# An encoder layer on one core: four raw weight buffers, products ordered by their operands, the first pass woven into the left factors, token tiles one by one at the ends

## The chip, the core and the metric

The kernel runs on one core of one Trainium2 chip. The metric is the device time of one execution in microseconds. Times are given for several runs of a kernel, beside one execution that the hardware profiler recorded, from which every row of a profile in this text comes. TensorE (PE) does the matmuls, VectorE (DVE) the elementwise work, ScalarE (ACT) activations and casts, GpSimd (POOL) little here, and SyncE (SP) issues nearly all DMA transfers on one queue, in its program order. Each engine executes its own stream in order.

## The reference

One layer of a token-mixing encoder over 512 tokens of 2048 features, in fp32. A vector `mod` of six rows of 2048 is made from `c`. Four mixers of 512 features each (a gated recurrence, a diagonal state space, stick-breaking attention, a delta rule) work on one projection; their outputs are projected, and a gated feed-forward block follows. What this text is about is the second half:

```python
shift1, scale1, gate1, shift2, scale2, gate2 = split(silu(c) @ ada_w + ada_b, 6)
...
mix = concatenate([o_a, o_b, o_c, o_d], -1) @ w_out               # 2048 x 2048
x = layer_norm(ALPHA * x + gate1 * mix, ln1_g, ln1_b)
h = x * (1 + scale2) + shift2
ffn = (silu(h @ ffn_w1) * (h @ ffn_w3)) @ ffn_w2                  # 2048 -> 5632 -> 2048
out = layer_norm(ALPHA * x + gate2 * ffn, ln2_g, ln2_b)
```

## The kernel before, in words

**Numbers.** Every fp32 operand of a matmul is split into a high part, rounded by ScalarE (`copy`, L101), and a low part, the difference taken by VectorE (`sub`, L104 with all two-operand VectorE work). `mm3` makes a product of two such operands from three matmuls (L92): high by high, low by high, high by low. So each weight block goes through four hands: an SP load of the raw values, ScalarE's rounding `wh`, VectorE's difference `wl`, and TensorE.

**Order.** The program is written with a tile framework. A tile comes from a pool with a fixed number of buffers, and the framework puts in the waits: a load into a buffer waits for the last reader of what was there. Its scheduler puts the instructions of each engine in an order that follows the order of the code, except that what stands under `tc.high_priority(offset=...)` may be taken earlier by that offset (`E.ahead` is 500 for the weights; `soon`, 1500, for evictions). Pools opened on `E.low`, `E.high` and `E.psum` are given back in the middle of the program; what is opened after that takes over their space, and waits tile by tile for it.

**Heads and output projection.** The first 1035 us hold the input projection, the mixers and two parts of the output projection (`w_out` inside `body`: "W1" and "W2" of the order string). The last part, four of sixteen groups of 128 rows, takes what the stick-breaking attention gives. Its weights `wr` are loaded (L1469), multiplied by the gate row `g1` (a broadcast load, L1167) and split into `woh` and `wol`; then for each token tile t of 128 tokens, 4 x 4 x 3 matmuls into `pd`, additions into `acc`, and a layer norm (L1205, L1207). These weights are prepared after `E.high.close()`, with `g1` in the pool `tp`.

**Factors.** The up projection uses Strassen's scheme in Winograd's form: tokens in halves of 256, the 2048 features in halves of 1024, and the weight columns of `ffn_w1` and `ffn_w3` as the two column blocks. `feature` turns `acc` with 128x128 transposes (L95) into feature-major tiles; the loop over j = 0..7 (128 features of each half) forms the left factors a11, a12, a22 and the sums s1..s4, each split in two, which stay in 56 slots of 128x512. After all eight the 16 normalised tiles are stored to `xn` (L1532).

**Up projection.** 11 blocks n of 512 columns. A block has two passes over j. The first pass loads three raw 128x512 blocks into a tile `wx` of 128x4x512 (L1558) and does 18 matmuls, p1 with a11, p3 with s4, p2 with a12. The second loads four, makes three differences of them in place on VectorE, splits all four (`wb`, then `wa`) and does 24 matmuls: p1 with s2, p4 with a22 (both on `wb`), p7 with s3, p5 with s1 (both on `wa`). `wx` has two buffers (pool `fx`), `wh` and `wl` four each (pool `fh`). The gate's pieces u, v, g1, g2 are evicted under `soon`. In the first pass of the next block, behind j = 3, `turned` transposes the gated product g, splits it into `gh` and `gl` of 128x2x512 (two buffers each) and stores them to the scratch `gd` (L1579).

**Down projection.** Two halves r of 1024 output columns; 44 row tiles f of `ffn_w2` in pairs; each pair loads one `wx` of 1 MB and four pieces of `gh`, `gl` back from `gd` (L1680 to L1686), and does 48 matmuls, 12 for each of four token tiles in four accumulators `pt`. The first and the last pair of a half run token tile by token tile, the others row tile by row tile. During r = 0 VectorE computes the row `gate2` (`gate_steps`), and `gate_rows` broadcasts it. During r = 1 the residual is prepared (`base`), and each token tile then gets its gate, sum, layer norm and stores (L1723).

## Time and profile before

| what | value |
|---|---|
| runs | 2649.61 us median of three (2642.85 to 2654.33) |
| profiled execution, its own time | 2645.44 us |
| its span, first to last instruction | 2643.7 us |
| mean granted TensorE clock | 0.972 |
| last matmul of "W2" to first of the last output projection's steady run | 1034.9 to 1057 us |
| last output projection and layer norm | to 1106.8 us |
| left factors | to 1139.6 us |
| block 0: first pass, second pass | to 1174.4, to 1223.8 us |
| blocks 1 to 10 of the up projection | to 2114.3 us |
| down projection | to 2605.1 us |
| tail | to 2643.7 us |

Rows of the profile are read so. A row of groups has the line, engine and operation, the tiles as out<-in, the shape, how many; then busy us, mean ns of one; then the idle time of the engine just before them and what ended most of it. A row of waits has who waited, for whom, the us in all, how often, and the mean. A row of stretches has the window, its length, the busy us and count of PE, PEld, DVE, ACT and POOL, the granted clock, the DMA engines' busy share and GB/s. A row of the timeline has the start in us, the length, and the instruction. "SPq" is the DMA-issuing queue of SyncE. Lines L93 and up of the changed kernel are those of before plus one.

### The profile page before, as it was taken

To read this page: it belongs to the slowest core of one execution; us is meant where nothing else is said; L and a number is where in the kernel's file an instruction comes from. 1 tells how busy PE (TensorE), PEld (TensorE's weight loads), DVE (VectorE), ACT (ScalarE), POOL (GpSimd) and SP (SyncE) were. 2 spreads that over 40 slices of the span, in tenths; PEclk is the share of its full clock that TensorE was granted. 3 is DMA by queue.
4 is the path that set the end of the run, shared out by engine and by line. 5 is a ranking of instruction groups with operands and counts; after the bars stand their busy time and mean duration, and the time that the engine had idled before them with its cause. 6 is when DMAs were issued, how large, how long until landed. Compare 5 with 4: busy or idle time off the path is not lost.

```text
span 2643.7 us, 33043 instructions
## 1 busy us (share of the span) xinstructions
PE 2470.3 (93%) x11890; PEld 1885.3 (71%) x11890; DVE 1738.4 (66%) x2629; ACT 930.1 (35%) x1350; POOL 71.8 (3%) x193
## 2 busy tenths in 40 slices
PE   8999999999999997879999999999999999999994
PEld 3557767767888785667677777776777678888883
DVE  3856985566798747867767776677777655436226
ACT  2435342322545633253334343443443321121110
POOL 3200000100000000000000000000000000000000
PEclk9999999999999998889999999999999999999997
DMA  9876225336545442245466556555655878859531
GB/s 288 264 230 200 82 75 152 117 107 208 167 132 156 151 140 88 88 136 191 164 203 201 186 174 203 193 180 189 203 191 184 289 265 312 291 192 330 196 110 64
DMA packets 334572, 481.81 MB, mean 182 GB/s; under 512 B 44259, under 2 KB 150973, under 8 KB 334409
## 3 DMA queue, kind: packets, MB, share of 16 engines
q1 hardware_dynamic: 331672, 479.00, 55.6%
q8 instruction: 93, 1.52, 0.2%
q10 hardware_dynamic: 2256, 0.67, 0.1%
q14 instruction: 71, 0.57, 0.1%
q0 software_dynamic: 480, 0.05, 0.0%
HBM read 445.51 MB, written 34.10 MB: 181 GB/s over the span
## 4 chain that ended last, share of the span: by engine, by line
PE 26%; DVE 16%; DMA 12%; issue 6%; ACT 4%; SPq 2%; DVEq 0%; ACTq 0%
PE pt L92 18%; DMA wx<-in_ffn_w_dram 12%; PE pd L92 6%; DVE wl L104 6%; DVE wx L104 5%; ACT wh L101 3%; SPq L1558 2%; PE p L92 1%; DVE g L104 1%; DVE v L104 1%; DVE acc L122 0%; DVE y L122 0%; DVE wr L104 0%; DVE st L1205 0%; DVE wol L104 0%
## 5 line engine op out<-in xcount | busy, mean ns | idle before, releaser
L104 DVE TENSOR_TENSOR wl<-wx,wh 128x1024 fp32r<-128x1024 f32 (+1 forms) x440 | 475.1, 1115 | 387.2 <-ACT wh L101 385.3
L101 ACT CAST wh<-wx 128x1024 fp32r<-128x1024 f32 (+1 forms) x440 | 409.0, 965 | 877.9 <-PE pt L92 332.2
L92 PE MATMUL pt<-wh,gh 128*128 128x512 f32 x704 | 274.7, 390 | 0.0
L92 PE MATMUL pt<-wl,gh 128*128 128x512 f32 x704 | 274.4, 390 | 0.0
L92 PE MATMUL pt<-wh,gl 128*128 128x512 f32 x704 | 274.3, 390 | 0.0
L101 ACT CAST wh<-wr 128x512 fp32r<-128x512 f32 x236 | 145.8, 620 | 339.1 <-PE pd L92 233.2
L104 DVE TENSOR_TENSOR wx<-wx 128x512 f32<-128x512 f32 (+1 forms) x264 | 229.2, 868 | 42.9 <-DMA wx<-in_ffn_w_dram 37.2
L122 DVE SCALAR_TENSOR_TENSOR acc<-aw,cact,acc 128x512 f32<-128x512 f32 x240 | 179.9, 749 | 102.8 <-DMA aw<-in_ada_w_dram 99.6
L104 DVE TENSOR_TENSOR wl<-wr,wh 128x512 fp32r<-128x512 f32 x236 | 162.3, 691 | 127.6 <-ACT wh L101 106.1
L92 PE MATMUL pd<-hh,wl 128*128 128x512 f32 x512 | 206.6, 403 | 3.5 <-DVE wl L104 3.3
L92 PE MATMUL pd<-hh,wh 128*128 128x512 f32 x512 | 206.1, 404 | 2.4 <-ACT hh L101 2.4
L92 PE MATMUL pd<-hl,wh 128*128 128x512 f32 x512 | 205.1, 401 | 0.0
L92 PE MATMUL p<-wh,hdh 128*128 128x512 f32 x352 | 149.7, 425 | 31.9 <-ACT wh L101 22.6
L92 PE MATMUL p<-wh,hch 128*128 128x512 f32 x352 | 141.5, 402 | 13.9 <-ACT wh L101 13.9
L92 PEld LDWEIGHTS pt<-wh,gh 128*128 128x128 f32 x704 | 132.5, 188 | 28.2 <-ACT wh L101 0.8
L92 PEld LDWEIGHTS pt<-wl,gh 128*128 128x128 f32 x704 | 132.5, 188 | 27.7
L92 PEld LDWEIGHTS pt<-wh,gl 128*128 128x128 f32 x704 | 132.5, 188 | 27.2
L92 PE MATMUL p<-wl,hdh 128*128 128x512 f32 x352 | 143.1, 407 | 4.0 <-DVE wl L104 4.0
L92 PE MATMUL p<-wl,hch 128*128 128x512 f32 x352 | 139.6, 396 | 2.2 <-DVE wl L104 2.2
L92 PE MATMUL p<-wh,hdl 128*128 128x512 f32 x352 | 141.4, 402 | 0.0
L92 PE MATMUL p<-wl,hbh 128*128 128x512 f32 x352 | 139.8, 397 | 0.0
L92 PE MATMUL p<-wh,hbl 128*128 128x512 f32 x352 | 138.6, 394 | 0.0
(495 smaller groups left out, 4283.2 us busy)
## 6 DMA issues: line engine op xcount, KB each, us to landing
wx<-in_ffn_w_dram SPq DMA_DIRECT2D x616, 256.0 KB, 4.1
aw<-in_ada_w_dram SPq DMA_DIRECT2D x384, 256.0 KB, 4.3
wr<-in_w_in_dram SPq DMA_DIRECT2D x184, 256.0 KB, 3.1
wx<-in_ffn_w_dram SPq DMA_DIRECT2D x44, 1024.0 KB, 5.4
gh<-gd SPq DMA_DIRECT2D x88, 256.0 KB, 5.4
gl<-gd SPq DMA_DIRECT2D x88, 256.0 KB, 5.2
wr<-in_w_out_dram SPq DMA_DIRECT2D x64, 256.0 KB, 2.8
gd<-gh SPq DMA_DIRECT2D x22, 512.0 KB, 5.4
```

Of the source, the lines that this page charges most:

```text
L92: return self.nc.tensor.matmul(out=out, lhsT=lhsT, rhs=rhs, start=start, stop=stop, **kw)
L101: self.nc.scalar.copy(out=out, in_=in_)
L104: self.nc.vector.tensor_tensor(out=out, in0=a, in1=b, op=op)
L122: self.nc.vector.scalar_tensor_tensor(out=out, in0=a, scalar=s, in1=b, op0=op0, op1=op1)
L1558: nc.sync.dma_start(out=x[:, s], in_=i[w][0, 128 * k : 128 * k + 128, T * n : T * n + T])
```

## The change

1. **Last output projection.** `g1` is taken from the pool `ap` instead of `tp`, and `E.high.close()` moves behind this projection. The pool `tp` has 34 buffers instead of 35, `wh` becomes a pool of the whole program, and a pool `w1` of one buffer is new.
2. **xn.** Each token tile is stored right after its norm, not after the factors.
3. **Block 0.** The first pass of block 0 is done inside the loop of factors, with single blocks of 128x512, in the accumulators `pd` and `pm` of the heads. Factors of j + 1 are written ahead of the products of j. The slots of the factors are the pools hp, pp, w1, af and wh.
4. **Up projection.** `wx` has four buffers instead of two. Of a second pass, `wa` is split before `wb`, and the products are p7, p5 (on `wa`), then p6, p4 (on `wb`), except at j = 7, where the latter go first. `gh` and `gl` are single 128x512 tiles with one buffer each, stored one by one, in two calls of `turned` behind j = 2 and j = 4. u, v, g1, g2 have one buffer each.
5. **Down projection.** At the start of a half the first two pairs run token tile by token tile; in the first half the last block's `turned` stands between the tiles t = 1 and t = 2. At the end, the last two pairs of the first half and the last four of the second run token tile by token tile. The pool `fz` has 9 buffers and gets more from w1 and wh; `base` is done for a column block at once.

The diff, cut to its core:

```diff
-NT = 35
+NT = 34
...
-        self.wh = self.open(self.low, "wh", 3)
+        self.wh = pool("wh", 3)
+        self.w1 = pool("w1", 1)
...
-    E.high.close()
-    late = ExitStack()
-    E.ax = E.open(late, "ax", 8, side="right")
...
-        g1 = bcast(E, E.gate[2][0:1, T * n : T * n + T], "g1")
+        g1 = E.ap.tile([128, T], F32, name=E.nm("g1"), tag="aw")
+        nc.sync.dma_start(out=g1, in_=E.gate[2][0:1, T * n : T * n + T].rearrange("o n -> (o n)").partition_broadcast(128))
...
             E.ts(acc[t][n], acc[t][n], mu, ALU.subtract, rs, ALU.mult)
+            nc.sync.dma_start(out=xn[t, n], in_=acc[t][n])
+    E.high.close()
...
-    slots = [E.hp] * 32 + [E.pp] * 16 + [E.ax] * 8
+    slots = [(E.hp, "t")] * 32 + [(E.pp, "t")] * 16 + [(E.w1, "t"), (E.af, "t")] + [(E.wh, "wh"), (E.wh, "wl")] * 3
...
-    for j in range(8):
+    def factors(j):
         f, e = feature(j), feature(j + 8)
...
-    E.fx = E.open(ffn_w, "fx", 2)
-    E.f2 = E.open(ffn_t, "f2", 2)
...
+    def single(s, j):
+        with tc.high_priority(offset=E.ahead):
+            x = E.sb("wx")
+            nc.sync.dma_start(out=x, in_=block(s, j, 0))
+            if j < 3:
+                hi, lo = (E.wh.tile([128, T], F32R, name=E.nm(m), tag=m) for m in ("wh", "wl"))
+            else:
+                hi, lo = E.sb("wh", dt=F32R), E.sb("wl", dt=F32R)
+            E.copy(hi, x)
+            E.sub(lo, x, hi.bitcast(F32))
+        return hi, lo
+
+    p1, p3 = [E.psd(), E.psd()], [E.psd(), E.psd()]
+    p2 = None
+    factors(0)
+    for j in range(8):
+        w = list(zip(*[single(s, j) for s in (0, 2, 3)]))
+        if j < 7:
+            factors(j + 1)
+        p2 = p2 or [E.psm(), E.psm()]
+        first_pass(j, p1, p2, p3, w)
...
+    E.fx = E.open(ffn_w, "fx", 4)
+    E.f2 = E.open(ffn_t, "f2", 1)
...
-            hi, lo = two(E.f2, "gh", "gh", F32R), two(E.f2, "gl", "gl", F32R)
-            E.copy(hi, ps)
-            E.sub(lo, ps, hi.bitcast(F32))
-            k = 4 * n + 2 * h
+        for q in range(2):
+            hi, lo = (E.f2.tile([128, T], F32R, name=E.nm(m), tag=m) for m in ("gh", "gl"))
+            E.copy(hi, ps[:, q])
+            E.sub(lo, ps[:, q], hi.bitcast(F32))
             for s, t in enumerate((hi, lo)):
-                nc.sync.dma_start(out=gd[k : k + 2, s].rearrange("f p t -> p f t"), in_=t.bitcast(F32))
+                nc.sync.dma_start(out=gd[4 * n + 2 * h + q, s], in_=t.bitcast(F32))
...
+                if j in (2, 4):
+                    turned(*before, j // 2 - 1)
...
-                wb = parts(x[:, 2:4])
                 wa = parts(x[:, 0:2])
-            product(p1, A[j]["s2"], wb, 0, False, j == 7, skip_group_check=True)
-            product(p4, A[j]["22"], wb, 1, j == 0, j == 7)
-            product(p7, A[j]["s3"], wa, 1, j == 0, j == 7)
-            product(p5, A[j]["s1"], wa, 0, j == 0, j == 7)
+                wb = parts(x[:, 2:4])
+            ab = [(p7, "s3", wa, 1), (p5, "s1", wa, 0)]
+            cd = [(p6, "s2", wb, 0), (p4, "22", wb, 1)]
+            for p, a, w, c in cd + ab if j == 7 else ab + cd:
+                product(banks(p), A[j][a], w, c, j == 0 and (n == 0 or p is not p6), j == 7, skip_group_check=p is p6)
...
+        pairs = [pair_w2(f, r) for f in (0, 2)]
+        pt = []
+        for t in range(4):
+            if r == 0 and t == 2:
+                for h in range(2):
+                    turned(*before, h)
+            pt.append(bank2("pt"))
+            for p in pairs:
+                mm_w2(pt[t], t, p)
...
+        ends = range(NFT - 4, NFT, 2) if r == 0 else range(NFT - 8, NFT, 2)
...
+        pairs = [pair_w2(f, r, f < NFT - 4) for f in ends]
+        for t in range(4):
+            for p in pairs:
+                mm_w2(pt[t], t, p)
+            with soon():
...
```

Three places show how this moves instructions. The first is VectorE's stream at the end of "W2", where the last output projection is prepared: `go` and `acc` are W2's evictions, `wr` the raw weights times the gate row `g`, `wol` their low parts. Before:

```order
L104 TENSOR_TENSOR go_9539<-pd_9459,g_2042_9455 128x512
L104 TENSOR_TENSOR go_9542<-pd_9460,g_2042_9455 128x512
L104 TENSOR_TENSOR acc_8940<-acc_8940,go_9539 128x512
L104 TENSOR_TENSOR acc_8943<-acc_8943,go_9542 128x512
L104 TENSOR_TENSOR wr_9553<-wr_9553,g_2063_9551 128x512
L104 TENSOR_TENSOR wr_9560<-wr_9560,g_2063_9551 128x512
L104 TENSOR_TENSOR wr_9567<-wr_9567,g_2063_9551 128x512
L104 TENSOR_TENSOR wol_9557<-wr_9553,woh_9556 128x512
L104 TENSOR_TENSOR wr_9574<-wr_9574,g_2063_9551 128x512
L104 TENSOR_TENSOR wol_9564<-wr_9560,woh_9563 128x512
```

The change has this at the same place:

```order
L105 TENSOR_TENSOR wl_9521<-wr_9518,wh_9520 128x512
L105 TENSOR_TENSOR wol_9644<-wr_9640,woh_9643 128x512
L105 TENSOR_TENSOR wol_9651<-wr_9647,woh_9650 128x512
L105 TENSOR_TENSOR wol_9658<-wr_9654,woh_9657 128x512
L105 TENSOR_TENSOR go_9536<-pd_9460,g_2042_9458 128x512
L105 TENSOR_TENSOR go_9539<-pd_9461,g_2042_9458 128x512
L105 TENSOR_TENSOR acc_8937<-acc_8937,go_9536 128x512
L105 TENSOR_TENSOR acc_8940<-acc_8940,go_9539 128x512
L105 TENSOR_TENSOR go_9542<-pd_9462,g_2042_9458 128x512
L105 TENSOR_TENSOR go_9545<-pd_9463,g_2042_9458 128x512
L105 TENSOR_TENSOR acc_8943<-acc_8943,go_9542 128x512
L105 TENSOR_TENSOR acc_8946<-acc_8946,go_9545 128x512
```

Before, all 16 multiplications by the gate row and all 16 low parts stand behind the last evictions of W2; now all 16 multiplications and 12 of the low parts stand far ahead in the stream, before the stick-breaking weights, three low parts just before the last evictions and one right behind them.

The second place is VectorE's stream in a second pass: `wx<-wx` are the differences in place (one of 128x1024 and two of 128x512 for each j), `wl<-wx,wh` the low parts, two for each j; equal numbers of `wx` belong to one j. Before:

```order
L104 TENSOR_TENSOR wl_15504<-wx_15495,wh_15503 128x1024
L104 TENSOR_TENSOR wl_15508<-wx_15495,wh_15507 128x1024
L104 TENSOR_TENSOR wx_15535<-wx_15535 128x512 x2
L104 TENSOR_TENSOR wl_15544<-wx_15535,wh_15543 128x1024
L104 TENSOR_TENSOR wl_15548<-wx_15535,wh_15547 128x1024
L104 TENSOR_TENSOR wx_15575<-wx_15575 128x1024
L104 TENSOR_TENSOR wx_15575<-wx_15575 128x512 x2
L104 TENSOR_TENSOR wl_15584<-wx_15575,wh_15583 128x1024
L104 TENSOR_TENSOR wl_15588<-wx_15575,wh_15587 128x1024
```

Now:

```order
L105 TENSOR_TENSOR wx_13970<-wx_13970 128x1024
L105 TENSOR_TENSOR wl_13899<-wx_13890,wh_13898 128x1024
L105 TENSOR_TENSOR wl_13903<-wx_13890,wh_13902 128x1024
L105 TENSOR_TENSOR wx_13970<-wx_13970 128x512
L105 TENSOR_TENSOR wx_14010<-wx_14010 128x1024
L105 TENSOR_TENSOR wl_13939<-wx_13930,wh_13938 128x1024
L105 TENSOR_TENSOR wx_13970<-wx_13970 128x512
L105 TENSOR_TENSOR wx_14010<-wx_14010 128x512
L105 TENSOR_TENSOR wl_13943<-wx_13930,wh_13942 128x1024
L105 TENSOR_TENSOR wx_14010<-wx_14010 128x512
L105 TENSOR_TENSOR wx_14050<-wx_14050 128x1024
L105 TENSOR_TENSOR wl_13979<-wx_13970,wh_13978 128x1024
```

Before, the differences of a j stand right ahead of its own low parts; now differences of one or two later j stand between.

The third place is TensorE's stream in the left factors: `pm<-ident,acc` are the transposes, `pd` and `pm` with `wh` or `wl` the products of the first pass of block 0. Before, it had nothing but transposes here:

```order
L95 MATMUL pm_10013<-ident,acc_8421 128x128
L95 MATMUL pm_10048<-ident,acc_8421 128x128
L95 MATMUL pm_10020<-ident,acc_8769 128x128
L95 MATMUL pm_10055<-ident,acc_8769 128x128
L95 MATMUL pm_10083<-ident,acc_8412 128x128
```

Now the products of one j stand between the transposes of two factors:

```order
L93 MATMUL pm_10128<-wh_10089,hbh_10059 128x512
L93 MATMUL pm_10128<-wh_10089,hbl_10060 128x512
L93 MATMUL pm_10128<-wl_10090,hbh_10059 128x512
L93 MATMUL pm_10129<-wh_10089,hbh_10059 128x512
L93 MATMUL pm_10129<-wh_10089,hbl_10060 128x512
L93 MATMUL pm_10129<-wl_10090,hbh_10059 128x512
L96 MATMUL pm_10166<-ident,acc_8415 128x128
L96 MATMUL pm_10166<-ident,acc_8418 128x128
L96 MATMUL pm_10166<-ident,acc_8421 128x128
```

Each j brings 18 matmuls to this place, 144 in all, which stood behind all the transposes before.

More of the change, by code (lines that the diff above doesn't have):

```diff
@@ L1563, in product @@
             v = slice(128 * b, 128 * b + 128)
[L1564 to L1577 removed]
+            mm3(E, p[b], (a[0][:, v], a[1][:, v]), (w[0][c], w[1][c]), first, last, **kw)
@@ new lines, in body @@
+    p1, p3 = [E.psd(), E.psd()], [E.psd(), E.psd()]
[7 more added lines that the diff above has]
+        first_pass(j, p1, p2, p3, w)
+    u0, v, g1 = two(E.ft, "u"), two(E.ft, "v"), two(E.ft, "g1")
+    with soon():
+        for b in range(2):
+            E.copy(u0[:, b], p1[b])
+            E.copy(v[:, b], p3[b])
+            E.add(g1[:, b], u0[:, b], p2[b])
+            E.act(g1[:, b], g1[:, b], AF.Silu)
@@ new lines, in body, with parts, quad @@
+    E.low.close()
+    E.psum.close()
+    E.fh = E.open(ffn_w, "fh", 4)
+    E.fx = E.open(ffn_w, "fx", 4)
+    E.f2 = E.open(ffn_t, "f2", 1)
+    E.p2 = E.open(last, "p2", 4, space=PSUM)
+    bank2 = lambda name: E.p2.tile([128, 2, T], F32, name=E.nm(name), tag="p")
+    banks = lambda p: (p[:, 0], p[:, 1])
+    def parts(src):
+        hi, lo = two(E.fh, "wh", F32R), two(E.fh, "wl", F32R)
+        E.copy(hi, src)
+        E.sub(lo, src, hi.bitcast(F32))
+        return banks(hi), banks(lo)
+    def quad(j, n, which):
+        x = E.fx.tile([128, 4, T], F32, name=E.nm("wx"), tag="wx")
+        for s in which:
+            nc.sync.dma_start(out=x[:, s], in_=block(s, j, n))
+        return x
@@ new lines, in gate_rows, with base @@
+        for n in range(4):
+            g2[n] = bcast(E, E.gate[5][0:1, T * n : T * n + T], "g2", "fz")
+    cols = lambda m, n, name, p: bcast(E, i[m][0:1, T * n : T * n + T], name, p)
+    def base(n):
+        g, b = cols("ln1_g", n, "lg", "hp"), cols("ln1_b", n, "lb", "hp")
+        E.ts(g, g, ALPHA, ALU.mult)
+        E.ts(b, b, ALPHA, ALU.mult)
+        for t in range(4):
+            a = E.sb("acc", pool=E.pp if n >= 2 else E.fz)
+            nc.sync.dma_start(out=a, in_=xn[t, n])
+            E.mul(a, a, g)
+            E.add(a, a, b)
+            if n < 2:
+                E.mul(y0[t][n], y0[t][n], g2[n])
+                E.add(y0[t][n], y0[t][n], a)
+                a = y0[t][n]
+            acc[t][n] = a
```

265 lines of the change are left out of this document (118 added, 147 removed).

## The prediction

> **What bounds the kernel now.** I read the page first, then a table of the stretches of the second half of the program, then the waits and the groups of its longest stretch.
>
> ```profile
> PE 2470.3 (93%) x11890; PEld 1885.3 (71%) x11890; DVE 1738.4 (66%) x2629; ACT 930.1 (35%) x1350; POOL 71.8 (3%) x193
> ...
> wx<-in_ffn_w_dram SPq DMA_DIRECT2D x616, 256.0 KB, 4.1
> ...
> gd<-gh SPq DMA_DIRECT2D x22, 512.0 KB, 5.4
> ```
>
> TensorE's 93% does not say that nothing can be won: its matmuls overlap, so a row of late ones still looks busy. The distance between the starts of two matmuls is the better measure. The chain of waits has a stretch in which TensorE alone sets the time:
>
> ```profile
> 2126.66 238.03 PE pt L92 x1050
> ```
>
> That is 238.03 / 1050 = 0.2267 us a matmul, which I use as its price. Now the stretches (busy us and count of PE, PEld, DVE, ACT, POOL, then clock, DMA share, GB/s):
>
> ```profile
> 900.00:1000.00 100.00, 96.03 (x446) 79.65 (x445) 52.56 (x83) 41.00 (x68) 0.00 (x0) 0.98 0.45 147
> 1035.20:1057.00 21.80, 3.29 (x5) 1.15 (x4) 21.80 (x38) 11.39 (x20) 0.00 (x0) 0.62 0.00 0
> 1057.00:1106.80 49.80, 46.62 (x202) 38.26 (x202) 38.75 (x96) 0.52 (x2) 0.00 (x0) 0.95 0.17 64
> 1106.80:1139.60 32.80, 13.99 (x52) 8.91 (x51) 30.65 (x67) 28.34 (x51) 0.00 (x0) 0.50 0.23 80
> 1139.60:1174.40 34.80, 34.63 (x144) 27.88 (x144) 18.50 (x21) 13.96 (x18) 0.00 (x0) 0.95 0.60 197
> 1174.40:1223.80 49.40, 46.43 (x193) 36.90 (x194) 39.10 (x41) 19.76 (x20) 0.00 (x0) 0.97 0.49 159
> 1223.80:2114.30 890.50, 835.60 (x3521) 640.26 (x3519) 646.17 (x658) 353.70 (x389) 0.00 (x0) 0.98 0.59 197
> 2114.30:2605.10 490.80, 484.30 (x2137) 400.05 (x2136) 203.23 (x239) 99.35 (x99) 0.00 (x0) 0.99 0.66 229
> 2605.10:2643.70 38.60, 0.17 (x1) 0.00 (x0) 35.15 (x88) 0.00 (x0) 0.00 (x0) 0.53 0.29 109
> ```
>
> The rows are: the heads, the preparation of the last output projection, that projection with its layer norm, the left factors, the first pass of block 0, its second pass, blocks 1 to 10 of the up projection, the down projection, and the tail after the last matmul. Three of them are VectorE's alone (1035 to 1057, 1106.8 to 1139.6, 2605 to the end). The longest is blocks 1 to 10: 3360 matmuls in 890.5 us, where 3360 x 0.2267 = 762 us would do.
>
> ```profile
> ACT wh L101 <- DVE wx L104: 288.7, 80, 4.8
> DVE wl L104 <- ACT wh L101: 183.4, 115, 5.1
> ACT wh L101 <- DMA wx<-in_ffn_w_dram: 154.6, 65, 8.0
> PEld p L92 <- ACT wh L101: 86.7, 147, 1.9
> PE p L92 <- ACT wh L101: 38.2, 82, 1.5
> ...
> PE p L92 <- DVE g L104: 9.0, 8, 1.5
> ...
> SPq L1558 <- DVE wl L104: 540.3, 155, 8.9
> ```
>
> Here is the ring: the load queue waits for VectorE's last read of a raw block (540 us), ScalarE waits for the load and for VectorE's differences, VectorE for ScalarE's rounding, and TensorE's weights for both. No engine in it is full (VectorE 646 of 890 us); two raw buffers make them take turns.
>
> **The change part by part.** A to F are in order of time. TensorE's matmuls are the same in number.
>
> **A, the last output projection's preparation.**
>
> ```profile
> 1034.93 0.39 PE L92 MATMUL pd<-wl,cath 128*128 128x512 f32 x1
> ...
> 1038.20 1.89 DVE L104 TENSOR_TENSOR wr<-wr,g 128x512 f32<-128x512 f32 x3
> ...
> 1058.02 0.63 PE L92 MATMUL pd<-woh,cath 128*128 128x512 f32 x1
> 1058.45 0.63 PE L92 MATMUL pd<-woh,catl 128*128 128x512 f32 x1
> ```
>
> Three of these multiplications take 1.89 us at 0.69 each, so they follow at 0.60. The 16 multiplications, 16 subtractions and 4 more for the left operand, 36 x 0.60 = 21.6 us, all stand behind the projection before, and TensorE gets four matmuls done from 1035.2 to 1057. In the order of the change all 16 multiplications and 12 of the 16 subtractions come earlier; of the last four, three stand before the last evictions and one behind. What covers them: in 900:1000 VectorE is busy 52.6 of 100 us. Gone are 21.8 less four matmuls (0.9), and some cold matmuls (0.43 apart at 1058 instead of 0.23). If the earlier place costs all that it saves the gain is 0; at best 22. I take 20, since the cover is more than twice the work: **-20**.
>
> **B, factors and first pass of block 0.**
>
> ```profile
> 1106.77 0.78 ACT L98 ACTIVATE hf<-pm,h2b,h2s 128x512 f32<-128x512 f32 x1 [49.28 <-PE pm L95]
> ...
> 1115.83 0.43 DVE L104 TENSOR_TENSOR hr<-hf,hf 128x256 f32<-128x256 f32 x1
> ...
> 1119.57 0.43 DVE L104 TENSOR_TENSOR hr<-hf,hf 128x256 f32<-128x256 f32 x1
> ```
>
> One factor step is 3.74 us of VectorE (1115.83 to 1119.57), eight are 30. Then the first pass takes until 1174.4: 67.6 us from the first factor. Now each step also splits three blocks, 3 x 0.60 on VectorE: 5.54 us, against 18 x 0.2267 = 4.1 us of TensorE and 8 transposes (52 of them fill 14.0 us at the half clock of that stretch, 0.27 each: at most 2.2 a step, half of it warm). So VectorE paces: 8 x 5.54 + 1.3 at the start + 4.1 for the last pass = 49.7; with 2.3 for handing on between three engines, 52: **-15.6**. Bounds: 49.7 (-18), and no overlap of the two at all (0). The 24 single loads stand behind the 16 xn stores on SP's queue, as the loads did before. [...]
>
> **C, second pass of block 0.** 49.4 us now against 192 x 0.2267 = 43.5. Its raw buffers take over the space of the tiles of B, so its first quad has to land (4.1), be subtracted and rounded (about 1.2 and 1.0) after B: 43.5 + 6.3 = 49.8. **0**, between -6 and +4 (one landing more).
>
> **D, blocks 1 to 10.**
>
> ```profile
> 1313.96 0.39 PE L92 MATMUL p<-wh,ha 128*128 128x512 f32 x1
> ...
> 1351.98 0.51 PE L92 MATMUL p<-wh,hdh 128*128 128x512 f32 x1 [0.30 <-ACT wh L101]
> ...
> 1402.51 0.63 PE L92 MATMUL p<-wh,ha 128*128 128x512 f32 x2
> ```
>
> First matmuls of a first pass, of its second pass, and of the next block: 38.0 and 50.5 us. At TensorE's price 8 x 18 x 0.2267 = 32.6 (35.0 with 16 transposes, 2.4) and 8 x 24 x 0.2267 = 43.5. What the feeders need for the second pass:
>
> ```profile
> L104 DVE TENSOR_TENSOR wl<-wx,wh 128x1024 fp32r<-128x1024 f32 x240 | 286.2, 1223 | 183.8 <-ACT wh L101 183.4
> ...
> L104 DVE TENSOR_TENSOR wx<-wx 128x512 f32<-128x512 f32 x160 | 110.7, 692 | 5.1
> ...
> L104 DVE TENSOR_TENSOR wx<-wx 128x1024 f32<-128x1024 f32 x80 | 97.7, 1222 | 33.0 <-DMA wx<-in_ffn_w_dram 32.9
> ...
> L95 PE MATMUL tr<-ident,g 128*128 128x128 f32 x16 | 2.4, 275 | 0.0
> ```
>
> (The last row is of one block, 1322 to 1410.) A quad is 3 x 1.22 + 2 x 0.69 = 5.0 us of VectorE against 24 x 0.2267 = 5.4 of TensorE. Before, its order was three differences and two subtractions in a row, each subtraction behind a rounding (183 us of waits); now differences of later quads stand between. Four buffers give a load three quads, 16 us, for its 4 issues and 4.1 us of landing. The demand, 56 loads of 256 KB per block, is 188 GB/s at 78 us a block; 229 were moved over the down projection. So TensorE paces: 76.2 + 2.4, and at each of two seams the wait for an eviction, 9.0 / 8 = 1.1: **81 us a block instead of 89.05, -80.5**. Bounds: -104 without any stall, 0 if the ring stays. I stay near the first, because all feeders fit in TensorE's time. The stores of gh and gl go from 4 of 512 KB to 8 of 256 a block, through one buffer instead of two: 4 pieces in a first pass of 35 us, each held for at most its landing of 5.4, 21.6 in all, fit.
>
> **E, down projection.**
>
> ```profile
> 2121.01 1.09 PE L95 MATMUL tr<-ident,g 128*128 128x128 f32 x4 [6.50 <-DVE g L104]
> ...
> 2364.61 1.07 PE L92 MATMUL gr<-acc,ones 128*32 128x512 f32 x8
> ```
>
> The last transposes wait 6.5 us for the gate; now two token tiles of the first two pairs (48 matmuls, 10.9 us) come first. 2112 x 0.2267 + 2.4 + 1.1 (eight small matmuls of the gate row) + 2 = 484.3 instead of 490.8: **-6.5**, between -8 and +8 (a landing and a half at the ends, where 32 tiles must be loaded).
>
> **F, tail.**
>
> ```profile
> 2597.15 1.29 DVE L104 TENSOR_TENSOR go<-pt,g 128x512 f32<-128x512 f32 x2 [11.51 <-PE pt L92]
> ...
> 2637.34 0.17 DVE L117 TENSOR_SCALAR lnr<-lnr 128x1 f32<-128x1 f32 x1
> ...
> 2638.87 1.41 DVE L122 SCALAR_TENSOR_TENSOR acc<-acc,lnr,lb 128x512 f32<-128x512 f32 x2
> ```
>
> Four token tiles now queue up behind 48 matmuls (10.9 us); VectorE takes from 2597.15 to 2640.3 for them, 10.8 us each. With four pairs to a tile the matmuls of one tile take 10.9 us, so VectorE just keeps step and one tile is left behind the last matmul. Its chain: six operations of 512 at 0.60, the aggregate 0.3, eight scalings at 0.66 (two take 1.41 at 0.75) and a dozen small ones at 0.2, with 0.3 for the start 11.9; and 3.4 from the end of the last VectorE operation (2640.3) to the span's end: 15.3 instead of 38.6: **-23.3**. Bounds -25 and, if VectorE lags 3 us a tile, -14.
>
> Sum: -20 - 15.6 + 0 - 80.5 - 6.5 - 23.3 = -145.9, from the profiled execution's 2645.4 (span 2643.7): 2499.5. Its time lies 4 us under the median of the three runs, which is inside their spread; I forecast **2500**. The heads, whose order shifts a little, get +-6.
>
> **Rivals.**
>
> 1. *VectorE and ScalarE keep the pace in D*: a second pass has 8% of room (5.0 of 5.4), and one rounding that comes late eats it. For it: 183 us of such waits. Against: other work now stands between. Half of D: 2500 + 40 = **2540**.
> 2. *The change does not do what it says in D*: the loads stay tied, by SP's one queue, in which a gd store that waits for its single gh buffer holds every load behind it, or ScalarE is held by that buffer with all roundings behind. For it: 5.4 us a store. Against: the old queue had such stores too, and its long waits are for VectorE. D is gone: **2580**.
> 3. *B runs at half clock.* Row for it: 0.50 granted in 1106.8:1139.6, and matmuls 0.43 apart at 1058. Then B is 144 x 0.43 + 64 x 0.27 = 79 instead of 52: **2527**. Against: TensorE has 4.1 us of matmuls in each 5.5. [...]
> 4. *Slower*: VectorE executes in order, and the multiplications of A now stand in the heads' time, before the stick-breaking weights; if they wait there for late gate rows or tiles, everything behind waits, and TensorE after it. The price is the wait itself; from 160 us it makes the kernel slower than before, say **2660**. Against: 900:1000 shows TensorE at 96 and VectorE half idle.
>
> **How the numbers follow.** Chances: forecast 0.60 (its own range 2465 to 2530, from the bounds of A, D and F), rival 1 0.17, rival 2 0.12, rival 3 0.08, rival 4 0.03. 2465 to 2555 holds the forecast's cases, rivals 1 and 3: 0.85 of the chance, less its edges. A measurement of this kernel can tell about 0.5% from no change; faster than that are all but rival 4 and some mishap on top of rival 2: 0.95, within it 0.02, slower 0.03.
>
> **What would show it.** A: no hole of 20 us before the last projection. B: about 52 us from the first factor to the second pass. D: starts of blocks 81 us apart, ScalarE's waits for DMA near zero. E: no wait of 6 us at the first down matmuls. F: 15 us after the last matmul. Wrong is the forecast if blocks stay above 86 us, or the heads end more than 10 us later.

## The result and the profile after

The changed kernel takes 2544.99 us, median of four runs (2540.67 to 2553.21), against 2646.23 us before in its company: a ratio of 0.9622, 95% interval 0.9579 to 0.9666. It is 101 us faster, where 146 were forecast; its profiled execution took 2540.67 us. The page's first rows, and the stretches that answer to those of before:

```profile
span 2539.0 us, 33233 instructions
...
PE 2422.7 (95%) x11890; PEld 1890.3 (74%) x11890; DVE 1733.9 (68%) x2665; ACT 946.5 (37%) x1386; POOL 77.2 (3%) x193
```

```profile
1042.40:1086.20 43.80, 43.80 (x195) 36.21 (x194) 35.47 (x83) 0.63 (x1) 0.00 (x0) 1.00 0.20 73
1086.20:1155.30 69.10, 46.31 (x210) 34.20 (x208) 53.25 (x110) 45.02 (x80) 0.00 (x0) 0.93 0.48 157
1155.30:1201.30 46.00, 45.50 (x192) 37.17 (x193) 40.83 (x44) 18.45 (x19) 0.00 (x0) 0.96 0.58 193
1201.30:1934.00 732.70, 710.24 (x3169) 581.77 (x3168) 576.76 (x613) 334.68 (x370) 0.00 (x0) 1.00 0.63 207
...
2028.90:2520.60 491.70, 485.69 (x2137) 399.95 (x2135) 221.63 (x297) 96.97 (x102) 0.00 (x0) 0.99 0.66 224
2520.60:2539.00 18.40, 0.21 (x1) 0.00 (x0) 13.77 (x32) 0.00 (x0) 0.00 (x0) 0.64 0.31 114
```

The rows are the last output projection, factors with the first pass of block 0, its second pass, blocks 1 to 9 (732.7 / 9 = 81.4 each), the down projection and the tail. Left out between is block 10, 1934.0 to 2028.9: 94.9 us, as against 81.4. By stage, in us of the two profiled executions:

| stage | before | after | moved | forecast |
|---|---|---|---|---|
| heads, to W2's last matmul | 1034.9 | 1042.4 | +7.5 | 0 (+-6) |
| A: from there to the first transpose of the factors | 66.7 | 43.8 | -22.9 | -20 |
| B: to the second pass of block 0 | 72.8 | 69.1 | -3.7 | -15.6 |
| C: second pass of block 0 | 49.4 | 46.0 | -3.4 | 0 |
| D: blocks 1 to 10 | 890.5 | 827.6 | -62.9 | -80.5 |
| E: down projection | 490.8 | 491.7 | +0.9 | -6.5 |
| F: tail | 38.6 | 18.4 | -20.2 | -23.3 |
| sum | 2643.7 | 2539.0 | -104.7 | -145.9 |

A and B are cut here at the first transpose of the factors (1101.6 us before, 1086.2 after). Cut at the first factor, as the forecast did it, B went from 67.6 to 64.1 us, where 52 were forecast.

The waits of blocks 1 to 9 (who waited for whom, us in all, how often, longest) show what became of the ring. The last figure of such a row is the longest wait, in the rows above too, where it was described as the mean:

```profile
ACT wh L102 <- PE p L93: 292.8, 215, 2.4
DVE wl L105 <- ACT wh L102: 93.3, 80, 1.5
DVE wx L105 <- DMA wx<-in_ffn_w_dram: 44.1, 35, 3.3
...
ACT wh L102 <- DMA wx<-in_ffn_w_dram: 1.5, 2, 0.7
```

ScalarE, which in blocks 1 to 10 waited 289 us for VectorE and 155 for loads, now in blocks 1 to 9 waits 293 us for TensorE and 1.5 for loads: ScalarE stands ready, and TensorE sets the time. VectorE's 44 us of waits for loads hardly reach it: its weights wait 0.8 us for `wl` there.

The runs had four questions: which part of the change carries D; what holds block 10; what B was short of; and where the heads lost 7.5 us. A and F were undone singly. The kernels of the experiments ran in four groups, each beside the kernel before, whose median there lies between 2644 and 2651 us; a difference of medians between two groups is therefore good to some 5 us, and the times of single stages, each read from one profiled execution, carry the readings.

### The profile page after: what moved, and what is told of

It is laid out like the page before. It is cut to its first block, busy times and chain, and to the rows that moved or that the text cites. A ratio compares the mean times of both kernels' runs of the same rounds, so it can differ in the third digit from the quotient of the medians.

```text
span 2539.0 us, 33233 instructions
## 1 busy us (share of the span) xinstructions
PE 2422.7 (95%) x11890; PEld 1890.3 (74%) x11890; DVE 1733.9 (68%) x2665; ACT 946.5 (37%) x1386; POOL 77.2 (3%) x193
## 3 DMA queue, kind: packets, MB, share of 16 engines
q8 instruction: 93, 1.52, 0.2%
## 4 chain that ended last, share of the span: by engine, by line
PE 53%; DVE 4%; DMA 3%; ACT 2%; issue 1%; SPq 0%; DVEq 0%; ACTq 0%
PE p L93 29%; PE pt L93 17%; PE pd L93 6%; DMA wx<-in_ffn_w_dram 2%; DVE wl L105 1%; ACT wh L102 1%; PE tr L96 1%; DVE gl L105 1%; DVE wx L105 0%; DVE acc L123 0%; SPq L1608 0%; DVE y L123 0%; DMA gd<-gl 0%; DVE st L1206 0%; ACT hf L99 0%
## 5 line engine op out<-in xcount | busy, mean ns | idle before, releaser
L102 ACT CAST wh<-wx 128x1024 fp32r<-128x1024 f32 (+1 forms) x444 | 421.5, 953 | 700.9 <-PE p L93 348.8
L105 DVE TENSOR_TENSOR wl<-wx,wh 128x1024 fp32r<-128x1024 f32 (+1 forms) x444 | 481.5, 1096 | 285.8 <-ACT wh L102 280.6
L93 PE MATMUL pt<-wh,gh 128*128 128x512 f32 x672 | 263.1, 392 | 6.0 <-DVE gl L105 6.0
L93 PE MATMUL pt<-wh,gl 128*128 128x512 f32 x672 | 262.6, 391 | 0.0
L93 PE MATMUL pt<-wl,gh 128*128 128x512 f32 x672 | 262.5, 391 | 0.0
L93 PE MATMUL p<-wh,hch 128*128 128x512 f32 x336 | 133.4, 397 | 13.4 <-ACT v L102 7.9
L93 PE MATMUL p<-wh,hbh 128*128 128x512 f32 x336 | 131.8, 392 | 8.5 <-DVE gl L105 8.5
L93 PE MATMUL p<-wh,hdh 128*128 128x512 f32 x352 | 137.1, 393 | 1.9 <-ACT u L102 1.0
L93 PE MATMUL p<-wl,hch 128*128 128x512 f32 x336 | 131.8, 392 | 0.5 <-DVE wl L105 0.5
L93 PE MATMUL p<-wl,hbh 128*128 128x512 f32 x336 | 131.6, 392 | 0.0
```

Of the source, the lines that this page charges most:

```text
L93: return self.nc.tensor.matmul(out=out, lhsT=lhsT, rhs=rhs, start=start, stop=stop, **kw)
L102: self.nc.scalar.copy(out=out, in_=in_)
L105: self.nc.vector.tensor_tensor(out=out, in0=a, in1=b, op=op)
```

## Experiments: what carries D

**Two raw buffers again.**

```diff
-    E.fx = E.open(ffn_w, "fx", 4)
+    E.fx = E.open(ffn_w, "fx", 2)
```

> The changed kernel with two raw buffers (pool fx) instead of four, all else as changed. If the number of raw buffers is what broke the ring of D, blocks 1 to 10 go back to about 88 us each from 82.7, and the time to about 2600. If the order of the products and of the differences did it, the blocks stay within 1 us of 82.7 and the time within 10 us of 2545.

2555.94 us, ratio 0.9672 (0.9648 to 0.9696): 11 us more than the change. Blocks 1 to 9 take 83.3 us each. With the new order, two buffers are nearly as good as four.

**The old order of a second pass.**

```diff
-                wa = parts(x[:, 0:2])
                 wb = parts(x[:, 2:4])
+                wa = parts(x[:, 0:2])
...
-            for p, a, w, c in cd + ab if j == 7 else ab + cd:
+            for p, a, w, c in cd + ab:
```

> The changed kernel with the old order in a second pass (wb split before wa, products p6, p4, p7, p5 at every j), still with four raw buffers. If the raw buffers carry D, blocks stay at 82 to 84 us and the time below 2560. If the order carries it, each second pass goes back towards 50 us from 45 and the time to about 2595.

2545.88 us, ratio 0.9628 (0.9612 to 0.9643), blocks of 81.6 us: no difference to the change. So with four buffers the order was not needed either, and neither run tells what carries D. The two had to be undone together.

**Both undone.** The two edits above in one kernel.

> The changed kernel with two raw buffers and the old order of a second pass together. Each alone cost little (blocks of 83.3 and 81.6 us). If either is enough to break the ring, both undone bring the blocks back to 87 to 89 us and the time to about 2610. If something else in the change does it (the transposed product taken in two calls and in single pieces, the evictions), the blocks stay below 85 us and the time below 2575.

2600.76 us, ratio 0.9815 (0.9788 to 0.9843). The eight blocks from 1294.0 to 1997.3:

```profile
1294.00:1997.30 703.30, 658.76 (x2817) 507.03 (x2817) 520.32 (x545) 284.30 (x328) 0.00 (x0) 1.00 0.59 192
```

703.3 / 8 = 87.9 us a block, against 88.9 before: the ring is back. What the rest of the change does in these blocks (transposes in two calls, single pieces, one buffer each) is 1 us a block at most, which two profiled executions can't tell from nothing (the run with the factors two steps ahead, below, shows why). Its waits beside those of the run with only the buffers undone, of stretches of eight blocks both; first both undone:

```profile
ACT wh L102 <- DVE wx L105: 220.1, 63, 5.1
DVE wl L105 <- ACT wh L102: 134.2, 82, 4.7
ACT wh L102 <- DMA wx<-in_ffn_w_dram: 126.0, 48, 7.3
PEld p L93 <- ACT wh L102: 64.7, 122, 1.7
```

And two buffers with the new order:

```profile
ACT wh L102 <- DVE wx L105: 155.0, 85, 5.0
ACT wh L102 <- DMA wx<-in_ffn_w_dram: 136.8, 59, 6.8
DVE wl L105 <- ACT wh L102: 89.2, 45, 4.3
```

With two buffers the loads come as late as ever (137 us of ScalarE's waits against 126). What the order takes away is the wait for the differences (220 to 155) and for the roundings (134 to 89), and TensorE's own 65 us of waiting for `wh`, of which 0.9 are left. That fits the code: `wa` needs only the first of three differences, so the first twelve matmuls of a j can be fed while the other two are made. That the twelve, and not VectorE's order as such, do it, was not separated.

**The order alone, in the kernel before.**

```diff
-                wb = parts(x[:, 2:4])
                 wa = parts(x[:, 0:2])
-            product(p1, A[j]["s2"], wb, 0, False, j == 7, skip_group_check=True)
-            product(p4, A[j]["22"], wb, 1, j == 0, j == 7)
-            product(p7, A[j]["s3"], wa, 1, j == 0, j == 7)
-            product(p5, A[j]["s1"], wa, 0, j == 0, j == 7)
+                wb = parts(x[:, 2:4])
+            ab = [(p7, "s3", wa, 1), (p5, "s1", wa, 0)]
+            cd = [(p1, "s2", wb, 0), (p4, "22", wb, 1)]
+            for p, a, w, c in cd + ab if j == 7 else ab + cd:
+                product(p, A[j][a], w, c, j == 0 and p is not p1, j == 7, skip_group_check=p is p1)
```

> The kernel before with only the new order of a second pass (wa split before wb, products p7, p5, p6, p4, at the last j the other way round); two raw buffers, all else as before. If the order alone breaks the ring, second passes fall from 51 to 43 to 46 us, blocks from 89 to 81 to 84, and the time to 2590 to 2600 (faster by 2%). If it needs the rest of the change, blocks stay above 87 and the time within 15 us of before.

2585.05 us, ratio 0.9749 (0.9723 to 0.9775). Nine blocks from 1217.6 to 1965.4:

```profile
1217.60:1965.40 747.80, 721.11 (x3169) 579.29 (x3169) 585.59 (x594) 326.19 (x351) 0.00 (x0) 1.00 0.62 203
```

747.8 / 9 = 83.1 us. A few lines that change no amount of work and no memory take 66 us from the kernel before, two thirds of what the whole change takes. The order and the buffers are two cures for one ring, and either alone is enough: the order alone in both kernels (83.1 and 83.3 us a block), the buffers alone in the changed kernel (81.6; in the kernel before they were not run alone). That both together bring more (81.4) is not clear of the differences between executions.

## Experiments: block 10 and the single store buffers

The timeline of SP's queue in the second pass of block 10 of the changed kernel, and VectorE's there:

```profile
1981.87 1.76 SPq L1608 DMA_DIRECT2D wx<-in_ffn_w_dram  x4
1983.72 0.38 SPq L1688 DMA_DIRECT2D gl<-gd  x1
...
1990.14 1.76 SPq L1608 DMA_DIRECT2D wx<-in_ffn_w_dram  x4
1992.00 0.38 SPq L1688 DMA_DIRECT2D gl<-gd  x1
1992.47 0.38 SPq L1688 DMA_DIRECT2D gh<-gd  x1
1992.90 0.42 SPq L1623 DMA_DIRECT2D gd<-gl  x1
```

```profile
1979.42 0.68 DVE L105 TENSOR_TENSOR gl<-tr,gh 128x512 fp32r<-128x512 f32 x1
...
1995.67 2.68 DVE L105 TENSOR_TENSOR wx<-wx 128x1024 f32<-128x1024 f32 x3 [4.96 <-DMA wx<-in_ffn_w_dram]
1998.88 0.69 DVE L105 TENSOR_TENSOR gl<-tr,gh 128x512 fp32r<-128x512 f32 x1 [0.53 <-DMA gd<-gl]
```

```profile
1999.72 0.76 PE L93 MATMUL p<-wh,hbh 128*128 128x512 f32 x1 [8.35 <-DVE gl L105]
```

The third piece `gl` of block 9 is made at 1979.4, but its store is issued only at 1992.9. Ahead of it in SP's queue stand loads of `gh` and `gl` for the down projection, and loads of two more quads `wx`, which in their turn wait for a raw buffer. From 1967 to 2002 the queue waits 9.5 us for VectorE's last reads of raw blocks and only 2.2 us for the slots of left factors that `gh` and `gl` take over. The fourth piece needs the buffer of the third, waits for that store, and holds the accumulator in which the product with a22 is to begin: TensorE starts it at 1999.7 after 8.35 us. Two holds end almost together there: on VectorE the fourth piece stands behind differences whose quad, issued at 1990.1 from the same queue, comes 5 us late, and the store's landing adds 0.5.

**These loads behind the stores.**

```diff
-        with tc.high_priority(offset=E.ahead):
-            x = E.fx.tile([128, 2, 2, T], F32, name=E.nm("wx"), tag="wx")
...
+        gg = []
+        with tc.high_priority(offset=E.ahead if r or f > 16 else 60):
+            for q in range(2):
+                hi, lo = E.sb("gh", dt=F32R, pool=E.hp), E.sb("gl", dt=F32R, pool=E.hp)
+                for s, t in enumerate((hi, lo)):
+                    nc.sync.dma_start(out=t.bitcast(F32), in_=gd[f + q, s])
+                gg.append((hi, lo))
+        with tc.high_priority(offset=E.ahead):
+            x = E.fx.tile([128, 2, 2, T], F32, name=E.nm("wx"), tag="wx")
```

> The changed kernel with the loads of gh and gl for the first pairs of the down projection placed later on SP's queue, behind the stores of the block before. If those loads, queued ahead of stores on which a single buffer waits, make the last second pass 61 us instead of 45, it goes to 46 to 48 and the time falls by 10 to 14 us. If the single buffers alone do it, or the banks, it stays above 58.

2531.02 us, ratio 0.9576 (0.9557 to 0.9596): 14 us less than the change. Block 10:

```profile
1947.10:2029.30 82.20, 79.01 (x353) 64.39 (x353) 64.74 (x69) 37.63 (x42) 0.00 (x0) 1.00 0.85 284
```

82.2 us instead of 94.9, like the others, while the DMA engines moved no less (284 GB/s; in the change 247 in the first pass and 288 in the second), so it is not the bandwidth. The place of these loads in the queue was the cause; the single buffers handed it on. Whether more buffers, with the loads left where they were, would have done as well was not run.

**Three edits read by stage.** The later loads; one rotating pool of three for `gh` and `gl`; and, for B, the low parts of block 0's first pass on GpSimd.

```diff
-    E.f2 = E.open(ffn_t, "f2", 1)
+    E.f2 = E.open(ffn_t, "f2", 3)
...
-            hi, lo = (E.f2.tile([128, T], F32R, name=E.nm(m), tag=m) for m in ("gh", "gl"))
+            hi, lo = (E.f2.tile([128, T], F32R, name=E.nm(m), tag="g") for m in ("gh", "gl"))
...
-            E.sub(lo, x, hi.bitcast(F32))
+            nc.gpsimd.tensor_tensor(out=lo, in0=x, in1=hi.bitcast(F32), op=ALU.subtract)
```

> Three local edits of the changed kernel, read by stage: the later loads of gh and gl as in the run before; gh and gl from one pool of three buffers instead of one buffer each; in the first pass of block 0 the low parts of the single weight blocks on GpSimd instead of VectorE. Blocks: if the single buffers still cost something, 82 falls towards 80. Start of the down projection: gaps of 8 us between its first matmuls fall to about 3 if the single buffers make them. B: if VectorE sets its pace (5.4 us of work and 1.1 of handing over in a step of 6.5), a step without the three low parts falls to about 5.3 us, ScalarE's pace, and B by 8 us; if the handing over between engines does, or GpSimd is slower than the step, B stays or grows. Time about 2520 if all three hold, 2530 if none but the first.

2521.08 us, ratio 0.9507 (0.9477 to 0.9538). Blocks 1 to 9 take 79.9 us instead of 82.0, and the down projection 486.5 instead of the 489.3 of the later loads alone (491.7 in the change). The changed kernel has these waits at its third and fourth token tile, whose accumulators the transposes had held:

```profile
2045.18 0.77 PE L93 MATMUL pt<-wh,gh 128*128 128x512 f32 x1 [3.49 <-DVE gl L105]
2054.78 0.70 PE L93 MATMUL pt<-wh,gh 128*128 128x512 f32 x1 [2.52 <-DVE gl L105]
```

So the single buffers do cost: about 2 us a block and 3 in the down projection. The three profiled kernels with three buffers have blocks of 79.9 to 80.1 us, the six with single ones and four raw buffers 81.4 to 83.0. B went the other way, from 69.1 to 77.8 us:

```profile
1109.66 4.80 POOL L1569 TENSOR_TENSOR wl<-wx,wh 128x512 fp32r<-128x512 f32 x3 [0.63 <-ACT wh L102]
```

GpSimd takes 4.0 to 4.8 us for three subtractions that take VectorE 1.89, and the steps grew from 6.5 to 7.7 us. Why, is read in the next section.

## Experiments: the pace of B

VectorE's timeline for one step of B in the changed kernel, and ScalarE's:

```profile
1120.95 0.43 DVE L105 TENSOR_TENSOR hr<-hf,hf 128x256 f32<-128x256 f32 x1 [0.33 <-ACT hf L99]
...
1122.90 0.42 DVE L105 TENSOR_TENSOR hs<-hf 128x256 f32<-128x256 f32 x1
1124.01 0.69 DVE L105 TENSOR_TENSOR hcl<-hs,hch 128x512 fp32r<-128x512 f32 x1 [0.69 <-ACT hch L102]
...
1125.22 1.89 DVE L105 TENSOR_TENSOR wl<-wx,wh 128x512 fp32r<-128x512 f32 x3
1127.43 0.43 DVE L105 TENSOR_TENSOR hr<-hf,hf 128x256 f32<-128x256 f32 x1 [0.33 <-ACT hf L99]
```

```profile
1123.35 0.62 ACT L102 CAST hch<-hs 128x512 fp32r<-128x512 f32 x1 [1.61 <-DVE hs L105]
1123.88 0.61 ACT L102 CAST hdh<-hr 128x512 fp32r<-128x512 f32 x1
1124.40 1.66 ACT L102 CAST wh<-wx 128x512 fp32r<-128x512 f32 x3
1125.96 1.44 ACT L99 ACTIVATE hf<-pm,h2b,h2s 128x512 f32<-128x512 f32 x2
```

A step is 6.48 us (1120.95 to 1127.43 from one `hr` to the next). VectorE has 5.4 of work in it, waits 0.69 until ScalarE has rounded a sum that VectorE made just before, and 0.33 for the next factor. But what sets the step is a ring in which the two engines take turns. VectorE needs 2.4 us from `hr` to the end of the last sum `hs` (1123.32). Then ScalarE rounds the sums and three weight blocks and makes the two halves `hf` of the next factor, 4.05 us without a pause (1123.35 to 1127.40), and the next `hr` needs the second `hf`. VectorE's low parts, `wl` among them, lie beside this ring.

The run with GpSimd bears this out. Without the three `wl` VectorE waits up to 2.1 us for `hf` in a step, and the step is no shorter:

```profile
1136.45 1.51 DVE L105 TENSOR_TENSOR ha<-hf,ha 128x256 fp32r<-128x256 f32 x1
...
1143.68 0.53 DVE L105 TENSOR_TENSOR hr<-hf,hf 128x256 f32<-128x256 f32 x1 [2.14 <-ACT hf L99]
```

ScalarE's part is 4.05 us there too (1139.60 to 1143.65). VectorE's part grew from 2.4 to 3.6 (1135.98 to 1139.57), nearly all of it in `ha`: 1.51 us instead of 0.42. It begins while a subtraction of GpSimd runs (1136.20 to 1137.68) and ends just behind it.

**Factors two steps ahead.**

```diff
     factors(0)
+    factors(1)
     for j in range(8):
         w = list(zip(*[single(s, j) for s in (0, 2, 3)]))
-        if j < 7:
-            factors(j + 1)
+        if j < 6:
+            factors(j + 2)
```

> The changed kernel with the factors written two steps ahead of the products of block 0 instead of one. If B is slow (64 us from the first factor to the second pass instead of the 52 forecast) because VectorE and ScalarE hand one step to and fro with nothing else to do meanwhile, a step falls from 7.15 to about 5.7 us and B by 8 to 10 us. If their work itself sets the pace (they are 53 and 45 us busy of 69), or TensorE's own stream does, B stays within 2 us.

2556.13 us, ratio 0.9666 (0.9647 to 0.9685). The steps stayed at 6.5 us, and B grew to 73.3, since a second factor now stands ahead of the first products. In ScalarE's order the next `hf` still stands behind the three weight roundings, and those behind the roundings of the sums, so a longer lead doesn't touch the ring.

B explains 4 of the 11 us that this run lost. Its blocks 1 to 9, which the edit doesn't touch and in which VectorE and ScalarE have the same instructions in the same order, took 83.0 us each instead of 81.4. So 1.6 us a block between two profiled executions need no cause in an edit.

**The sums first.** With the later loads and the three buffers of above, and VectorE for all low parts:

```diff
         m = {}
+        E.add(s1, a21, a22)
+        E.sub(s2, s1, a11)
+        E.sub(s4, a12, s2)
+        E.sub(s3, a11, a21)
         one = slot("ha")
...
         m["12"], m["22"] = halves(e, "hb")
-        E.add(s1, a21, a22)
-        E.sub(s2, s1, a11)
-        E.sub(s4, a12, s2)
-        E.sub(s3, a11, a21)
         m["s3"], m["s4"] = halves(s, "hc")
```

> The changed kernel with the later loads of gh and gl, with one pool of three buffers for gh and gl, all low parts on VectorE again, and the four sums of a factor written ahead of its splits, so that VectorE has two other operations between a sum and its low part. If the 1.1 us of handing over between VectorE and ScalarE in each step of B is what the forecast left out, a step falls from 6.5 to about 5.6 us and B from 69 to about 63 (from the first transposes to the second pass). If another chain sets the step, B stays within 2 us of 69. The two other edits give 42.2 us for a second pass and 46 or less for the last one. Time about 2507 if B gains, 2512 if not.

VectorE's timeline of a step:

```profile
1128.22 0.42 DVE L105 TENSOR_TENSOR hs<-hf,hr 128x256 f32<-128x256 f32 x1
1128.56 0.69 DVE L105 TENSOR_TENSOR hbl<-hf,hbh 128x512 fp32r<-128x512 f32 x1
1129.34 0.69 DVE L105 TENSOR_TENSOR hcl<-hs,hch 128x512 fp32r<-128x512 f32 x1
...
1132.76 0.42 DVE L105 TENSOR_TENSOR hr<-hf,hf 128x256 f32<-128x256 f32 x1 [0.32 <-ACT hf L99]
```

`hbl` (0.60) now stands behind the last sum instead of ahead of it. VectorE's part of the ring is 1.76 us (1126.88 to 1128.64), ScalarE's still 4.05, and the step 5.88 (1126.88 to 1132.76); the wait of 0.69 is gone too. The stages, B, block 10 and the down projection:

```profile
1093.80:1158.80 65.00, 46.30 (x210) 34.38 (x208) 53.05 (x110) 45.33 (x80) 0.00 (x0) 0.92 0.51 166
...
1924.50:2004.20 79.70, 78.14 (x353) 64.59 (x352) 64.35 (x69) 37.52 (x41) 0.00 (x0) 1.00 0.87 295
2004.20:2489.20 485.00, 482.28 (x2137) 397.93 (x2136) 220.87 (x297) 96.83 (x102) 0.00 (x0) 1.00 0.68 232
```

B is 65.0 us instead of 69.1, blocks 1 to 9 79.9, block 10 79.7, the down projection 485.0. The kernel takes 2505.44 us, ratio 0.9460 (0.9437 to 0.9483). The four lines that were moved here stood in this order in the kernel before; the change had turned them round, at 0.6 us a step. The cut diff above leaves them out.

## Experiments: A, F and the heads

**A undone.**

```diff
+    E.high.close()
     grp = (8, 9, 10, 11)
...
-        g1 = E.ap.tile([128, T], F32, name=E.nm("g1"), tag="aw")
-        nc.sync.dma_start(out=g1, in_=E.gate[2][0:1, T * n : T * n + T].rearrange("o n -> (o n)").partition_broadcast(128))
+        g1 = bcast(E, E.gate[2][0:1, T * n : T * n + T], "g1")
...
-    E.high.close()
     late, ffn_w, ffn_t, last = ExitStack(), ExitStack(), ExitStack(), ExitStack()
```

> The changed kernel with the gate row of the last output projection taken from the pool tp again, behind the end of the pools of the heads. If A is what the forecast says, the hole before the last projection comes back, its time from 1042.4 to the first transposes goes from 43.8 to 65 us, and the kernel is slower by about 20 us. If the heads' loss of 7.5 us (their last matmul at 1042.4 instead of 1034.9) is the price of the earlier multiplications, the heads end at 1035 again, and the kernel is slower by only 13 us.

2568.01 us, ratio 0.9690 (0.9665 to 0.9715): 23 us more. From 1041.9 to the first transpose at 1109.1 it is 67.2 us, and TensorE's waits for the last weights are back:

```profile
1048.36 0.80 PE L93 MATMUL pd<-woh,cath 128*128 128x512 f32 x1 [6.08 <-ACT cath L102]
...
1054.98 0.79 PE L93 MATMUL pd<-woh,cath 128*128 128x512 f32 x1 [4.02 <-ACT woh L102]
```

W2's last matmul stays at 1041.9, so the multiplications that A puts into the heads cost them nothing that shows, and the 7.5 us are elsewhere.

**Two pairs instead of four at the end.**

```diff
-        ends = range(NFT - 4, NFT, 2) if r == 0 else range(NFT - 8, NFT, 2)
+        ends = range(NFT - 4, NFT, 2)
```

> The changed kernel with two instead of four pairs token tile by token tile at the end of the second half. If the tail is short because the 10.9 us of matmuls of four pairs cover the 10.8 us of VectorE's work on a token tile, two pairs (5.4 us) let VectorE lag by 5.4 us at each of three tiles: the tail goes from 18.4 to about 31 to 34 us and the time up by 13 to 16. If one pair more than before would have done, or the tail is short for another reason, it stays below 22.

2565.00 us, ratio 0.9693 (0.9661 to 0.9725), 20 us more than the change, of which the stretch behind the last matmul explains 13.7:

```profile
2526.40:2558.50 32.10, 0.17 (x1) 0.00 (x0) 28.01 (x71) 0.00 (x0) 0.00 (x0) 0.53 0.27 99
```

32.1 us instead of 18.4: F's mechanism and size hold. The other 6 us are not explained: in the profiled executions the heads are 2.0 us and blocks 1 to 9 together 3.5 us longer than the change's, in instructions that the edit leaves as they were.

**One buffer less in the kernel before.**

```diff
-NT = 35
+NT = 34
```

> The kernel before with 34 buffers in the pool tp instead of 35, all else as before. If the missing buffer costs the heads their 7 us (their matmuls are 4 to 5 us later from 320 us on, far ahead of the moved multiplications), the last matmul of W2 moves from 1034.9 to 1040 or later here too, and the time is 5 us longer or so. If not, it stays within 2 us of 1034.9, and the cost is elsewhere in the change.

2656.81 us, ratio 1.0032 (1.0016 to 1.0048), 10 us more. W2's last matmul of this kernel:

```profile
1045.70 0.39 PE L92 MATMUL pd<-wl,cath 128*128 128x512 f32 x1
```

It came at 1034.93 before: 10.8 us. A pool of 35 buffers that loses one, far from any line that the forecast looked at, is the loss of the heads. In the three profiled kernels with 35 buffers this matmul comes at 1032.1 to 1034.9, in the eleven with 34 at 1041.8 to 1050.3.

**The buffer given back.** The kernel of the sums, with 35 buffers; the space comes from opening the pool w1 after the heads, and g2 from a pool of its own.

```diff
-NT = 34
+NT = 35
...
-        self.w1 = pool("w1", 1)
...
+    under = ExitStack()
+    E.w1 = E.open(under, "w1", 1, side="right")
     E.af = E.open(late, "af", 1, side="right")
...
+    E.fg = E.open(ffn_t, "fg", 1)
...
-            g2 = two(E.ft, "g2")
+            g2 = two(E.fg, "g2")
```

> The last kernel (later loads of gh and gl, one pool of three buffers for them, sums first) with 35 buffers in the pool tp again: the pool w1 is opened only after the heads, and g2 of the gated product has a pool of its own, so that the space is enough. If the missing buffer is what the heads lose, they end at about 1035 to 1042 instead of 1042 to 1050, the gap to the kernel before in the heads closes, and the time falls by 5 to 10 us to about 2497. If the heads' loss belongs to the moved preparation of the last output projection, nothing changes (2505).

2495.50 us, ratio 0.9442 (0.9422 to 0.9463): 10 us less than the kernel it comes from by the medians and 5 by the ratios, whose intervals overlap, and the lowest of all. W2's last matmul, which came at 1050.07 in the kernel of the sums:

```profile
1032.05 0.39 PE L92 MATMUL pd<-wl,cath 128*128 128x512 f32 x1
```

## Why the prediction was right and where it was not

The direction and the place of the gain were right: the last projection's hole, the blocks and the tail make 106 of 105 us. The time, 2545, lies in the stated range, 45 above the forecast, but outside the forecast's own range, 2465 to 2530. It was covered only because rivals 1 and 3 (2540 and 2527) were added to that range, and neither of them came: to this extent the range was luck. By its steps:

- **A** was -20 and measured -22.9; undone, +23. Right.
- **B** was -15.6 and measured -3.7. The step that failed is "So VectorE paces: 8 x 5.54". VectorE's work in a step was priced rightly (5.4), but it doesn't set the pace: the ring of VectorE's sums (2.4) and ScalarE's roundings and halves (4.05) does, and ScalarE's part was not priced. The seven steps from the first `hr` (1093.10) to the last (1140.40) take 47.3 us (the last three 6.5 each, the second 9.9), where 38.8 were forecast. The step of 3.74 was read from rows in which the sums come first; the changed code has them behind the splits, which the forecast did not use. Putting them back gave 0.6 a step. About 3 us more are at the end: 14.9 from the last `hr` to the second pass, where 11.9 were forecast (a step, the last pass and the 2.3 for handing on). There ScalarE evicts u and v and applies the gate's activation before it rounds the first quad. Rival 3 is out; the rows are below.
- **C** was 0, measured -3.4; its wait for the first quad lies ahead of its first matmul, in what was just counted in B.
- **D**: 81 us a block were forecast and blocks 1 to 9 took 81.4. The reason given was half right. Both named causes, more buffers and other work between a rounding and its reader, are real, but the text added them up as one cure, and each is enough without the other. That 81 met 81.4 is partly luck, since the single store buffers, which were to "fit" at no cost, take about 2 us of each block. Rival 1 did not come: ScalarE waits for TensorE. Rival 2, stores that hold the loads in one queue, came in one block of ten and the other way round: loads of `gh` and `gl`, drawn forward by their priority, held the stores, and block 10 took 94.9 us, 13.9 of the 17.6 us that D misses. The step that failed is "each held for at most its landing of 5.4": the store that held block 10 took 13 us from the piece's making to its issue, behind what stood ahead of it in the queue, and only then nearly 6 to land.
- **E** was -6.5, measured +0.9. The wait for the gate's transposes is gone, but the same single buffers make two waits, of 3.5 and 2.5 us, behind the new place of the transposes, each with some matmuls 0.43 us apart after it, where those that follow are 0.23 apart. With three buffers the down projection took 485.0, where 484.3 were forecast.
- **F** was -23.3, measured -20.2. VectorE needs 11.85 us a token tile (its `go` start at 2500.07, 2511.91 and 2523.76) against 10.9 of matmuls, and lags 3 us by the last tile; "just keeps step" was 1 us a tile too good.
- **Heads**: +7.5, outside the +-6 that were given to their order, and from neither their order nor rival 4's multiplications: the 35th buffer, which the text never priced. The first line of the diff is the one that it left out.

Heads (7.5), B (11.9), block 10 and 0.4 in each other block (17.6), E (7.4) and F (3.1), less A (2.9) and C (3.4), make the 41 us between 145.9 and 104.7. Three of these, the heads' buffer, the queue of block 10 with the single pieces, and 0.6 us per step of B, were mended in the last kernel, which lands at 2495.5.

Rival 3 was B at half clock. No row of the kernel before showed the clock of a load like B's, so that the rival would fail was the author's estimate. The steady products of B, and its start, up to the first product:

```profile
1098.30:1148.60 50.30, 42.15 (x186) 31.52 (x186) 39.35 (x78) 34.43 (x65) 0.00 (x0) 0.96 0.38 121
1086.20:1098.30 12.10, 2.31 (x17) 1.59 (x15) 9.64 (x27) 5.49 (x10) 0.00 (x0) 0.75 0.56 188
```

The granted clock is 0.96 in the products, in which TensorE has 42.2 us of work in 50.3, and 0.75 in the 12.1 us before, in which it has 2.3. The 0.50 on which the rival rested was granted in a stretch with 14.0 us of work in 32.8.

Open are: why the 35th buffer is worth 10 us (without it the matmuls of the heads fall behind in steps from 300 us on, and which tile waits was not followed up); why the heads end at 1049 to 1050 in the three kernels with the later loads and 34 buffers, and 3 to 8 us earlier in the eight others with 34; which half of the new order, the split or the products, breaks the ring; and the last 6 us of the run with two pairs at the end.

## What to carry to other kernels

Where a weight block goes through several engines in turn, first order the products by which of their operands is ready first: that cost nothing here and, in the kernel before, brought two thirds of the gain by itself, and more buffers were a second cure for the same ring, not a further one. Where two engines hand tiles to and fro, look for the ring before adding up the work of either: taking a third of VectorE's work away (1.89 of 5.4 us) did not shorten a step, and moving one operation behind the last sum did (from 6.48 us to 5.88). When a store gets a single buffer, read from the order of its queue what stands ahead of the store: in block 10 that was 13 us of the hold, and the landing nearly 6. And price each buffer that a change takes from a pool elsewhere: one of 35 was worth 10 us.
